# Regrouping tokens 256/512/256 with the samples in the first group, and plain float32 for half of the dense up-projections

## Chip, cores and metric

One core of a Trainium2 chip runs the whole program. The metric is device time in microseconds, the median of three runs. Engines are called TensorE (PE, with its weight loads PEld), VectorE (DVE), ScalarE (ACT), GpSimd (POOL) and SyncE (SP, which issues most DMAs).

## The reference

One inference step of a one-layer decoder for a prompt of 1024 tokens and for 32 samples (8 sequences of 4 new tokens), all in float32, with the same weights. A token mixer (a gated delta rule with a recurrent state, and three groups of dilated window attention), attention over a memory of 256 entries, and PEER, a layer of 16384 experts of which each token picks 8 x 16:

```
def layer(h, conv_buf, s0, wins, kv, g_mix, ...):
    mix, ... = token_mixer(rmsnorm(h, g_mix), conv_buf, s0, wins, w_in, ..., w_out)
    h = h + mix
    h = h + mem_attend(rmsnorm(h, g_memq), kv, w_mq, w_mo)
    h = h + peer(rmsnorm(h, g_ffn), w_pq, sub_keys, expert_u, expert_v)
...
    # peer, for a block of tokens xb
    q = (xb @ w_pq).reshape(PEER_BLOCK, PEER_HEADS, 2, PEER_DHALF)
    s = einsum('thpc,hpnc->thpn', q, sub_keys);  sv, si = top_k(s, 16)
    cand = sv[:, :, 0, :, None] + sv[:, :, 1, None, :];  cv, ci = top_k(cand, 16)
    eid = i1 * PEER_NKEYS + i2;  gate = softmax(cv)
    hid = gelu(einsum('thkd,td->thk', expert_u[eid], xb))
    out = einsum('thk,thkd->td', gate * hid, expert_v[eid])
```

The samples have own states: a recurrent matrix and convolution rows for each sequence, window caches of 128, 512 and 2048 positions, and a memory cache. They are outputs too, shifted by the new tokens.

## The kernel before

Tokens go through in three groups: 384, 384 and 256 prompt tokens; the 32 samples ride with the second group (SG = 1, n = 416 columns). For each group `base(gi)` runs norm, projections (activations are kept transposed, 128 model rows by n tokens), convolutions, delta blocks of 128 tokens, the three window groups, `w_out`, memory attention and the norm before PEER; then `peer_route` picks experts (top 16 twice for each of 8 heads, on VectorE, one round for each block of tokens). Group 0 splits each operand into a high and a low float32r part (`split`: one ScalarE copy, one VectorE subtraction) and multiplies three products; groups 1 and 2 use plain float32 matmuls. `wtile` loads a weight pair of 2 x 512 KB and calls `sprinkle`, which advances the generator `self.gate` by some steps.

PEER is done in two ways. Sparse tokens (group 0, and 192 tokens of group 2) gather their expert rows: `experts` issues one indirect DMA of 128 rows of 4 KB for each slot on GpSimd, and VectorE takes a dot product (L1257) or adds a scaled row (L1406). That is 576 slots for `expert_u` and 576 for `expert_v`, four blocks of 128 and one half block (64 tokens folded to 128 rows, `peer_rest`). They are traced at the very end; `mm` notes an anchor instruction on VectorE after each `rate` columns of matmul (float32 counted four times), and `paced` ties one gather step behind each anchor, so that the gathers spread over the rest of the kernel. RATES give the columns per anchor by stage.

Dense tokens (group 1 with its samples, and 64 of group 2: ND = 480) go through all experts. `gate_matrix` builds, for 32 tokens at a time, a matrix of gates over 128 x 128 experts from two one-hot matrices (L1299 and L1306 on VectorE, L1305 and L1308 on ScalarE, four matmuls for four tokens, L1313 copies them out) and writes it to DRAM (`gscr`). `expert_up` computes Gelu of one group of 128 experts for all dense tokens: load 512 KB, split, 24 matmuls of 480 columns (three products of eight chunks), Gelu (L1330). 60 of the 128 groups are done ahead and parked in DRAM (`uscr`); the loop in `dense` reads those back or computes the others, multiplies by gates, splits, and does 24 matmuls for the down-projection into seven PSUM accumulators. `finish_T` adds, norms and writes.

A scheduler orders the traced instructions on each engine by the order of tracing, and pulls later ones forward where an engine would be idle and their buffers (SBUF tags and PSUM tags with a fixed number of slots) are free. The order is fixed when the kernel is built; each engine then runs its own in order. Of the eight PSUM banks `ps` has 2, `tp` (transposes) 2, `po` 1 and `dl` 3.

Order before: base 0 with the memory's K/V, route 0; base 1; route 1 and then the gate matrix of group 1, stepped on by the weight loads of base 2 (STEPS); base 2; then, in `dense`, the split operand is loaded, the 60 early up-projections are traced with route 2 and the gate matrix of the 64 tokens stepped between them (PACE); then the dense loop.

Of the kernel before, what the change touches and what calls it, by code (L numbers as in the profile page):

```python
# [27 lines left out]
GI = 4  # L28
STEPS = (2, 4)
PACE = (1, 1, 1, 1, 1, 1, 1, 1, 1, 1, 1, 1, 1)  # L30
RATES = (4000, 3900, 2000, 3700)
EARLY = 60
NDT = 9
# [4 lines left out]
TD = 4  # L38
GROUPS = ((0, 384), (384, 384), (768, 256))
SG = 1  # L40
EX = 64
N1 = 384 + NS
ND = N1 + EX
KEPT = 256 - EX
COPIES = 3
# [86 lines left out]
class Kern:  # L132
# [36 lines left out]
    def p(self, shape, tag="ps", dt=F32):  # L169
        self.uid += 1  # L170
        bufs = {"ps": 2, "tp": 2, "po": 1, "dl": 3}[tag]
        return self.ps.tile(list(shape), dt, tag=tag, name=f"{tag}_{self.uid}", bufs=bufs)
# [18 lines left out]
    def setup(self):  # L191
        nc, I = self.nc, self.I
        self.x0 = self.t((P, KD, GROUPS[0][1]), "O", 1)
        self.load_x(0, self.x0)
        cf = self.const.tile([P, CF_N], F32, name="cf")
        nc.sync.dma_start(cf, I["cf"])
        self.C = {n: cf[:, o:o + w] for n, (o, w) in CF_OFF.items()}
        cb = self.const.tile([P, CB_N], BF16, name="cb")
        nc.gpsimd.dma_start(cb, I["cb"])
        self.CB = {n: cb[:, o:o + w] for n, (o, w) in CB_OFF.items()}  # L200
        identb = self.const.tile([P, P], BF16, name="identb")
        nc.vector.tensor_copy(identb, self.C["ident"])
        self.identb = identb
        gains = self.const.tile([P, 5, KD], F32, name="gains")
        nc.sync.dma_start(gains, I["gains"])
# [24 lines left out]
        self.hscr = self.dr.tile([SEQ, D], F32, name="hscr")  # L230
        self.fscr = self.dr.tile([SEQ, D], F32, name="fscr")
# [31 lines left out]

    def operand(self, a, n, kn=KD, tags=(("fr", 1, 2), ("acc", 1, 2), ("vzs", 1, 2), ("oh", 1, 2))):
        if self.gi:
            return ([a[:, k] for k in range(kn)],)
        hi, lo, k = [], self.t((P, kn, n), "A", 1, F32R), 0
        for tag, bufs, m in tags:
            m = min(m, kn - k)
            if m:  # L270
                x = self.t((P, m, n), tag, bufs, F32R)
                self.split(a[:, k:k + m, :n], x, lo[:, k:k + m, :n])
                hi += [x[:, j] for j in range(m)]
                k += m
        return hi, [lo[:, k] for k in range(kn)]
# [10 lines left out]
    def sprinkle(self, k):  # L286
# [3 lines left out]
        self.calls += 1  # L290
        for _ in range(k if k > 100 else STEPS[self.calls > 9]):
            next(self.gate, None)
# [129 lines left out]
    def delta_in(self, gi, L, n, h, a, stc, ncv, qk_all, vz_all, vzs, ssp):  # L422
# [14 lines left out]
        if gi == 0:  # L437
            for b in range(nb):
                nc.tensor.transpose(zp[:, b], zT[:, b * P:(b + 1) * P], C["ident"])
        for b in range(nb + smp if gi else 0):  # L440
# [720 lines left out]
    def peer_route(self, gi, L, n, f, hres):  # L1161
# [5 lines left out]
        self.spare = "dtm", NDT, 512  # L1167
        eid, gate = self.t((P, 8, nt, 16), "eid", 2, I32), self.t((P, nt, 8, 16), "gate", 2)
        for h in range(8):
# [98 lines left out]

    def gate_dense(self, route):
        nc, C = self.nc, self.C  # L1270
        yield from route
        yield from self.gate_matrix(self.picks[1], 0, 0, lambda: [self.t((P, P, UT), "C", 1)])

    def gate_extra(self):
        yield from self.gate_matrix(self.picks[2][1:], P - EX, N1 // UT, lambda: [self.t((P, P // 2, UT), x, 1) for x in "OA"])

    def gate_matrix(self, picks, skip, out, tiles):
        nc, C = self.nc, self.C
        for eid, gate in picks:
# [12 lines left out]
            yield  # L1292
            for sub in range(skip // UT, m // UT):
                st = tiles()
                nu = P // len(st)
# [21 lines left out]
                out += 1  # L1317

    def expert_up(self, e, fh, fl):
        nc = self.nc  # L1320
# [12 lines left out]
    def dense(self, route):  # L1333
        nc, I = self.nc, self.I
        fl, fh = self.t((P, KD, ND), "B", 1, F32R), self.t((P, KD, ND), "C", 1, F32R)
        last = self.t((P, ND), "vzs", 1)
        for k in range(KD):
            x = self.tmp((P, ND))
            nc.sync.dma_start(x, self.tscr[0, :, k])
            self.split(x, fh[:, k], fl[:, k])  # L1340

        self.rate = RATES[2]
        side = chain(route, self.gate_extra())
        early = {e: i for i, e in enumerate(e for e in range(P) if e * EARLY // P != (e + 1) * EARLY // P)}
        for e, i in early.items():
            for _ in range(PACE[i // 4] if i % 4 == 0 and i // 4 < len(PACE) else 0):
                next(side, None)
            nc.sync.dma_start(self.uscr[i], self.expert_up(e, fh, fl))
        for _ in side:
            pass  # L1350
        self.rate = RATES[3]
        gs = self.t((P, 2, ND // UT, GI, UT), "A", 1)
        gs = [gs[:, j] for j in range(2)]
        wx = self.t((P, 2, 2, ND), "O", 1, F32R)
        accs = [self.p((P, ND), tag) for tag in ("tp", "tp", "dl", "dl", "dl", "po", "ps")]

# [65 lines left out]
    def finish_T(self, h):  # L1422
        t0, L = GROUPS[1]
        self.norm_T(self.ks(h), 4, ND, self.ks(h))
        for b in range(L // P):
            self.rows(h, b * P, P, self.O["y_p"], t0 + b * P)
        self.rows(h, L, NS, self.O["y_s"], 0)
        if EX:
            self.rows(h, N1, EX, self.O["y_p"], SEQ - EX)

    def store_rows(self, src, gi, scr):
        t0, L = GROUPS[gi]
        for c0 in range(0, KEPT if gi else L, P):
            self.rows(src, c0, min(P, KEPT - c0) if gi else P, scr, t0 + c0)

# [10 lines left out]
    def base(self, gi):  # L1446
# [30 lines left out]
        if smp:  # L1477
            self.zq = [c[:, 3072:].rearrange("p (b t) -> p b t", b=8)]
        def windows(i):
# [35 lines left out]
        self.norm_T(self.ks(h), 3, n, self.ks(f))  # L1515
        if gi:
            o, c0 = (0, 0) if gi == 1 else (N1, KEPT)
            for x, y in enumerate((f, h)):
                if c0 < n:
                    nc.sync.dma_start(self.tscr[x, :, :, o:o + n - c0], y[:, :, c0:])  # L1520
        if gi != 1:
            self.store_rows(f, gi, self.fscr)
# [4 lines left out]
    def peer(self, gi, sel):  # L1527
        nc, O = self.nc, self.O
        t0, L = GROUPS[gi]
        for b in range((KEPT if gi else L) // P):  # L1530
            r0 = t0 + b * P
# [7 lines left out]
    def peer_rest(self, eid, gate):  # L1539
        nc = self.nc  # L1540
        m, r0 = KEPT % P, SEQ - P
        parts = P // m
# [16 lines left out]
        self.finish(acc[:m], self.O["y_p"][r0:r0 + m])  # L1559

    def run(self):
# [3 lines left out]
        for gi in range(3):  # L1565
            route = self.base(gi)
            if gi == 2:
                self.sprinkle(1000)
                self.finish_T(self.dense(route))
                break  # L1570
            if gi == 0:
                for _ in route:
                    pass
                self.work, self.anchors = 0, []
            else:
                self.calls = 0
                self.rate = RATES[1]
                self.gate = self.gate_dense(route)
        self.paced(chain(self.peer(0, self.picks[0]), self.peer(2, self.picks[2]), self.peer_rest(*self.picks[2][1]) if KEPT % P else ()))

# [99 lines left out]
```

## Time and profile before

| | |
|---|---|
| runs | 4074.78 us median, 4065.51 to 4086.79 |
| span of the profiled execution | 4081.0 us, the only time that it has of its own |
| TensorE busy | 3619.0 us, 89% |
| VectorE busy | 2938.5 us, 72% |
| ScalarE, GpSimd busy | 36% each |
| DMA | 1101.38 MB, mean 270 GB/s |
| HBM | 1025.37 MB read, 117.02 MB written |

Busy times are shares of the span. Matmuls overlap in the record, so the duration of one is longer than the distance to the next; where pace matters, the length of a run of equal matmuls is divided by their number. A plain float32 product appears as two instructions, a float32r product as one. The granted clock is a share of TensorE's full 2.4 GHz.

### The profile page before, as it was taken

The page shows a single profiled execution, that of the slowest core. Times are in us where ns is not written, and L with a number is a line of the kernel's source. Part 1 is how long each engine was busy: PE and PEld are TensorE (multiplying, and loading weights), DVE is VectorE, ACT ScalarE, POOL GpSimd, SP SyncE. Part 2 cuts the span into 40 slices and gives each one's busy share as a digit, 9 for nine tenths or more (in the row PEclk, how much of TensorE's full clock was granted, in tenths as well). Part 3 has the DMA queues.
Part 4 walks back from the last instruction along what each step waited for, and adds up shares of the span by engine and source line. Part 5 has one row for each costly group of instructions (what it writes and reads, how often), then busy time and mean ns, then how long its engine had stood idle before and what let it go on. Part 6 is the DMA issues. An engine that isn't in the chain of part 4 may idle for free.

```text
span 4081.0 us, 54174 instructions
## 1 busy us (share of the span) xinstructions
PE 3619.0 (89%) x18530; PEld 2976.6 (73%) x18530; DVE 2938.5 (72%) x6731; ACT 1470.6 (36%) x3278; POOL 1477.9 (36%) x1317
## 2 busy tenths in 40 slices
PE   8999988888999878774799887899969999999999
PEld 8988878666777634443677776788858888888887
DVE  4422338876575655789977887899768888887886
ACT  4434344333223011211245687223443333333333
POOL 0000000253334545454334443444544444444442
PEclk9998899789878988787788898999989999999998
DMA  6532554376668988886577888999999999999995
GB/s 219 188 117 92 189 196 146 123 254 206 230 229 298 334 331 310 296 297 201 189 237 267 290 321 330 327 349 330 348 323 336 342 342 340 340 339 321 338 332 198
DMA packets 383525, 1101.38 MB, mean 270 GB/s; under 512 B 40528, under 2 KB 147728, under 8 KB 379536
## 3 DMA queue, kind: packets, MB, share of 16 engines
q0 software_dynamic: 168736, 614.54, 42.5%
q1 hardware_dynamic: 214512, 483.37, 33.9%
q8 instruction: 147, 2.41, 0.2%
q14 instruction: 130, 1.06, 0.1%
HBM read 1025.37 MB, written 117.02 MB: 280 GB/s over the span
## 4 chain that ended last, share of the span: by engine, by line
PE 49%; DMA 18%; DVE 14%; issue 10%; POOL 4%; ACT 4%; POOLq 0%; SPq 0%; DVEq 0%; ACTq 0%
PE ps L148 29%; PE dl L148 11%; DMA gat<-expert_u,eid 5%; DMA gat<-expert_v,eid 5%; PE tp L148 4%; POOL gat L1248 4%; PE po L148 3%; DVE gat L1257 2%; DVE acc L1406 2%; DMA gat<-expert_v,e 1%; DMA O<-cmv 1%; PE tp L846 1%; DVE tk L1155 1%; DMA gscr<-C 1%; DVE tmp L419 1%
## 5 line engine op out<-in xcount | busy, mean ns | idle before, releaser
L1248 POOL DMA_INDIRECT gat<-expert_u,eid x512 | 625.1, 1221 | 819.1 <-DVE hid L1257 569.0
L1248 POOL DMA_INDIRECT gat<-expert_v,eid x512 | 627.7, 1226 | 771.8 <-DVE acc L1406 420.3
L1257 DVE CUSTOM_DVE_ANT_0 gat<-gat,fr 128x1024 f32<-128x1024 f32 x576 | 697.1, 1219 | 220.5 <-DMA gat<-expert_u,eid 209.2
L1406 DVE SCALAR_TENSOR_TENSOR acc<-gat,hid,acc 128x1024 f32<-128x1024 f32 x576 | 737.2, 1280 | 146.1 <-DMA gat<-expert_v,eid 128.9
L148 PE MATMUL dl<-dtm,dtm 128*128 128x128 f32 (+3 forms) x2336 | 328.2, 292 | 36.6 <-ACT C L1313 18.1
L148 PE MATMUL ps<-C,w 128*128 128x416 f32 x768 | 309.8, 562 | 43.2 <-DMA w<-w_pq 31.6
L148 PEld LDWEIGHTS dl<-dtm,dtm 128*128 128x128 f32 (+2 forms) x2336 | 307.7, 206 | 54.9 <-ACT C L1313 20.5
L148 PE MATMUL dl<-O,dtm 128*128 128x480 f32 x1152 | 286.3, 379 | 0.0
L148 PEld LDWEIGHTS ps<-C,w 128*128 128x128 f32 x768 | 156.7, 209 | 175.0 <-issue 127.3
L1266 ACT ACTIVATE dtm<-w 128x512 fp32r<-128x512 f32 x288 | 178.0, 629 | 269.7 <-PE dl L148 183.6
L148 PE MATMUL ps<-C,wk 128*128 128x480 f32 x1024 | 249.3, 385 | 21.2 <-ACT C L1266 12.7
L148 PE MATMUL ps<-C,zz 128*128 128x480 f32 (+1 forms) x1088 | 263.1, 379 | 1.4 <-DVE zz L1267 1.4
L1266 ACT ACTIVATE wk<-wv 128x1024 fp32r<-128x1024 f32 x128 | 135.8, 1061 | 332.9 <-PE ps L148 219.8
L148 PE MATMUL ps<-B,wk 128*128 128x480 f32 x1024 | 244.9, 381 | 0.2 <-DVE B L1267 0.2
L148 PEld LDWEIGHTS dl<-O,dtm 128*128 128x128 f32 x1152 | 216.6, 188 | 33.5
L148 PE MATMUL tp<-O,dtm 128*128 128x480 f32 x768 | 208.3, 386 | 32.1 <-ACT O L1266 30.1
L148 PEld LDWEIGHTS ps<-C,wk 128*128 128x128 f32 x1024 | 191.2, 190 | 56.4 <-ACT C L1266 13.6
L148 PEld LDWEIGHTS ps<-C,zz 128*128 128x128 f32 x1088 | 204.1, 188 | 32.3 <-DVE zz L1267 1.8
L1267 DVE TENSOR_TENSOR dtm<-w,dtm 128x512 fp32r<-128x512 f32 x288 | 197.0, 688 | 41.4 <-PE dl L148 16.8
L148 PE MATMUL ps<-A,w 128*128 128x256 f32 (+1 forms) x768 | 197.4, 415 | 21.2 <-ACT tmp L406 13.7
L148 PEld LDWEIGHTS ps<-B,wk 128*128 128x128 f32 x1024 | 193.8, 189 | 30.2 <-DVE B L1267 0.9
L148 PE MATMUL ps<-O,dtm 128*128 128x480 f32 x768 | 210.5, 379 | 0.2 <-DVE vzs L1394 0.2
(479 smaller groups left out, 6665.4 us busy)
## 6 DMA issues: line engine op xcount, KB each, us to landing
wv<-expert_uT SPq DMA_DIRECT2D x128, 512.0 KB
w<-expert_v SPq DMA_DIRECT2D x128, 512.0 KB
w<-w_in SPq DMA_DIRECT2D x102, 512.0 KB
s_win<-cache_win SPq DMA_DIRECT2D x64, 512.0 KB
A<-gscr SPq DMA_DIRECT2D x32, 960.0 KB
gscr<-C SPq DMA_DIRECT2D x13, 2048.0 KB
w<-w_pq SPq DMA_DIRECT2D x48, 512.0 KB
uscr<-tmp SPq DMA_DIRECT2D x60, 240.0 KB
```

Of the source, the lines that this page charges most:

```text
L148: x = self.nc.tensor.matmul(out, lhsT, rhs, **kw)
L419: nc.vector.scalar_tensor_tensor(av, xv(j), cw[:, ch, j:j + 1], av, op0=ALU.mult, op1=ALU.add)
L846: nc.tensor.transpose(tp[:r, c, :], e[:lq, j, o:o + r], C["ident"][:lq, :lq])
L1155: nc.vector.match_replace(out=w, in_to_replace=vals[:, 0:8], in_values=src, imm_value=-3.0e38)
L1248: return self.nc.gpsimd.indirect_dma_start(out=dst, out_offset=None, in_=src, in_offset=bass.IndirectOffsetOnAxis(ap=idx, axis=0))
L1257: nc.vector.tensor_tensor_reduce(out=u, in0=u, in1=fr, scale=1.0, scalar=0.0, op0=ALU.mult, op1=ALU.add, accum_out=hid[:, s:s + 1])
L1266: nc.scalar.activation(hi, x, AF.Copy)
L1267: nc.vector.tensor_tensor(lo, x, hi.bitcast(F32), op=ALU.subtract)
L1406: nc.vector.scalar_tensor_tensor(acc, v, c[:, s:s + 1], acc, op0=ALU.mult, op1=ALU.add)
```

## The change

Groups become 256, 512 and 256, the samples ride with the first (n = 288), and only group 1 is dense: 512 tokens, no samples, nothing of group 2. The sparse tokens are group 0's two blocks, the 32 samples (folded to 128 rows of 32 slots) and group 2's two blocks: 544 slots.

Each group's picks get own buffers (`eid0`, `gate0`, ...). `sprinkle` advances route 1 by one step at each weight load. The gate matrix of group 1 is no longer stepped on in base 2; it is traced after base 2 and route 2, in tiles `B` and `O` + `A` by turns.

Of the 128 up-projections 64 instead of 60 are done ahead, and these by a new function, `expert_fill`: plain float32, 8 products of 512 columns, no splits, from the operand `F` that group 1 left in tile `C`, into an own PSUM bank `fl` (taken from `tp`, which keeps one), with Gelu written over the weight tile. The first 24 use the SBUF tag `vzs` with one slot, the others `wv` with two. They are traced after route 2 and the whole gate matrix. The split operand, in `B` and `C`, is loaded after them.

```
-STEPS = (2, 4)
-PACE = (1, 1, 1, 1, 1, 1, 1, 1, 1, 1, 1, 1, 1)
-RATES = (4000, 3900, 2000, 3700)
-EARLY = 60
+RATES = (4000, 4600, 1500, 3700)
+EARLY = 64
+FILL = 24
...
-GROUPS = ((0, 384), (384, 384), (768, 256))
-SG = 1
-EX = 64
-N1 = 384 + NS
-ND = N1 + EX
-KEPT = 256 - EX
+GROUPS = ((0, 256), (256, 512), (768, 256))
+SG = 0
+ND = GROUPS[1][1]
...
-        bufs = {"ps": 2, "tp": 2, "po": 1, "dl": 3}[tag]
+        bufs = {"ps": 2, "tp": 1, "fl": 1, "po": 1, "dl": 3}[tag]
...
-    def operand(self, a, n, kn=KD, tags=(("fr", 1, 2), ("acc", 1, 2), ("vzs", 1, 2), ("oh", 1, 2))):
+    def operand(self, a, n, kn=KD, tags=(("fr", 1, 3), ("acc", 1, 3), ("oh", 1, 2))):
...
-        for _ in range(k if k > 100 else STEPS[self.calls > 9]):
+        for _ in range(max(k, 1)):
             next(self.gate, None)
...
-        eid, gate = self.t((P, 8, nt, 16), "eid", 2, I32), self.t((P, nt, 8, 16), "gate", 2)
+        eid, gate = self.t((P, 8, nt, 16), f"eid{gi}", 1, I32), self.t((P, nt, 8, 16), f"gate{gi}", 1)
...
-    def gate_matrix(self, picks, skip, out, tiles):
+    def gate_matrix(self, picks):
+        out = 0
...
-            for sub in range(skip // UT, m // UT):
-                st = tiles()
+            for sub in range(m // UT):
+                st = [self.t((P, P // 2, UT), x, 1) for x in "OA"] if out % 2 else [self.t((P, P, UT), "B", 1)]
...
+    def expert_fill(self, e, tag, bufs):
+        nc = self.nc
+        u = self.t((P, KD, P), tag, bufs)
+        nc.sync.dma_start(u, self.I["expert_uT"][e])
+        q = self.p((P, ND), "fl")
+        for k in range(KD):
+            nc.tensor.matmul(q, u[:, k], self.F[:, k], start=k == 0, stop=k == KD - 1)
+        x = u.rearrange("p k e -> p (k e)")[:, :ND]
+        nc.scalar.activation(x, q, AF.Gelu_apprx_tanh)
+        return x
...
     def dense(self, route):
         nc, I = self.nc, self.I
+        self.rate = RATES[2]
+        side = chain(route, self.gate_matrix(self.picks[1]))
+        early = {e: i for i, e in enumerate(e for e in range(P) if e * EARLY // P != (e + 1) * EARLY // P)}
+        for _ in side:
+            pass
+        for e, i in early.items():
+            nc.sync.dma_start(self.uscr[i], self.expert_fill(e, *(("vzs", 1) if i < FILL else ("wv", 2))))
+        self.rate = RATES[3]
         fl, fh = self.t((P, KD, ND), "B", 1, F32R), self.t((P, KD, ND), "C", 1, F32R)
...
-        for e, i in early.items():
-            for _ in range(PACE[i // 4] if i % 4 == 0 and i // 4 < len(PACE) else 0):
-                next(side, None)
-            nc.sync.dma_start(self.uscr[i], self.expert_up(e, fh, fl))
-        for _ in side:
-            pass
-        self.rate = RATES[3]
...
-        accs = [self.p((P, ND), tag) for tag in ("tp", "tp", "dl", "dl", "dl", "po", "ps")]
+        accs = [self.p((P, ND), tag) for tag in ("tp", "fl", "dl", "dl", "dl", "po", "ps")]
...
+        if gi == 1:
             for x, y in enumerate((f, h)):
-                if c0 < n:
-                    nc.sync.dma_start(self.tscr[x, :, :, o:o + n - c0], y[:, :, c0:])
-        if gi != 1:
+                nc.sync.dma_start(self.tscr[x], y)
+            self.F = f
+        else:
             self.store_rows(f, gi, self.fscr)
...
-        self.paced(chain(self.peer(0, self.picks[0]), self.peer(2, self.picks[2]), self.peer_rest(*self.picks[2][1]) if KEPT % P else ()))
+        self.paced(chain(self.peer(0, self.picks[0]), self.peer_rest(*self.picks[0][-1]), self.peer(2, self.picks[2])))
```

## Rows read from the trace of the kernel before

**Rows 1.** The page, busy time of each engine with its share of the span.

```profile
PE 3619.0 (89%) x18530; PEld 2976.6 (73%) x18530; DVE 2938.5 (72%) x6731; ACT 1470.6 (36%) x3278; POOL 1477.9 (36%) x1317
```

**Rows 2.** Busy time by stretch; length, then engines, granted clock, DMA share, GB/s.

```profile
0.00:606.00 606.00, 561.20 (x3267) 511.69 (x3267) 207.76 (x384) 264.21 (x640) 11.47 (x33) 0.92 0.48 168
606.00:890.00 284.00, 237.85 (x1195) 190.40 (x1196) 240.49 (x1058) 105.13 (x219) 72.54 (x98) 0.87 0.50 164
890.00:1390.00 500.00, 453.14 (x2808) 360.90 (x2809) 320.32 (x659) 123.68 (x420) 217.99 (x206) 0.87 0.73 253
1390.00:1660.00 270.00, 220.84 (x880) 128.04 (x880) 156.38 (x239) 43.76 (x114) 125.43 (x104) 0.84 0.90 329
1660.00:2080.00 420.00, 291.88 (x1203) 208.35 (x1202) 372.47 (x1433) 90.15 (x239) 199.92 (x166) 0.81 0.72 243
2080.00:2516.00 436.00, 376.43 (x2351) 318.05 (x2351) 344.63 (x796) 293.29 (x760) 174.69 (x146) 0.87 0.80 284
2516.00:2988.00 472.00, 428.31 (x2066) 368.02 (x2064) 406.31 (x935) 196.31 (x346) 220.32 (x176) 0.97 0.93 337
2988.00:4050.00 1062.00, 1025.86 (x4650) 872.13 (x4651) 881.09 (x1219) 343.03 (x526) 455.53 (x388) 0.98 0.93 331
4050.00:4081.00 31.00, 23.49 (x120) 19.06 (x118) 9.05 (x18) 11.01 (x20) 0.00 (x0) 0.67 0.20 64
```

**Rows 3.** Line L1248, the gathers: duration min/median/max, first and last start.

```profile
L1248 POOL DMA_INDIRECT gat<-expert_u,eid x512: 935/970/3978, 648.6 to 3319.0; - x171
...
L1248 POOL DMA_INDIRECT gat<-expert_v,e x64: 939/1115/2283, 3854.3 to 4021.2; - x64
```

**Rows 4.** Groups of instructions: busy us, mean ns; idle before, releaser.

```profile
L1257 DVE CUSTOM_DVE_ANT_0 gat<-gat,fr 128x1024 f32<-128x1024 f32 x576 | 697.1, 1219 | 220.5 <-DMA gat<-expert_u,eid 209.2
L1406 DVE SCALAR_TENSOR_TENSOR acc<-gat,hid,acc 128x1024 f32<-128x1024 f32 x576 | 737.2, 1280 | 146.1 <-DMA gat<-expert_v,eid 128.9
```

**Rows 5.** The chain that ended last: start us, us, what.

```profile
1218.38 5.74 PE tp L148 x50
...
2864.04 31.21 PE ps L148 x144
```

**Rows 6.** Busy time of the stretch of group 0's delta blocks and windows.

```profile
133.00:457.00 324.00, 312.03 (x1938) 275.91 (x1938) 93.10 (x209) 129.57 (x411) 0.61 (x4) 0.89 0.34 115
```

**Rows 7.** Busy time where the samples' parts ran in group 1.

```profile
1130.00:1200.00 70.00, 63.12 (x457) 51.86 (x457) 53.04 (x114) 15.25 (x51) 25.45 (x27) 0.76 0.62 214
1200.00:1240.00 40.00, 36.95 (x243) 29.17 (x242) 29.25 (x55) 6.95 (x27) 20.59 (x24) 1.00 0.95 358
1340.00:1380.00 40.00, 27.71 (x183) 23.61 (x184) 25.80 (x44) 1.92 (x9) 23.96 (x25) 0.91 0.90 339
1484.00:1570.00 86.00, 51.01 (x308) 24.62 (x308) 39.71 (x72) 16.47 (x47) 32.34 (x28) 0.74 0.93 345
```

**Rows 8.** Timeline of TensorE: start us, us, runs of equal matmuls.

```profile
1034.73 7.85 PE L148 MATMUL ps<-C,w 128*128 128x416 f32 x22
...
2330.81 2.84 PE L148 MATMUL dl<-dtm,dtm 128*128 128x128 f32 x24
```

**Rows 9.** Groups of instructions of the gate matrix, 480 tokens.

```profile
L1306 DVE TENSOR_SCALAR dtm<-cb,i 128x128 f32<-128x128 bf16 x480 | 137.4, 360 | 5.1 <-PE dl L148 4.7
...
L1305 ACT ACTIVATE dtm<-cb,i 128x128 f32<-128x128 bf16 x360 | 112.9, 394 | 1.8 <-PE dl L148 1.7
...
L1299 DVE TENSOR_TENSOR dtm<-cb,i 128x512 f32<-128x512 bf16 x30 | 20.5, 685 | 2.2 <-ACT i L1291 2.2
```

**Rows 10.** Line L1330, the Gelu of an up-projection.

```profile
L1330 ACT ACTIVATE tmp<-ps x128: 545/572/587, 2568.3 to 4037.3; 128x480 f32<-128x480 f32 x128
...
L1330 ACT ACT_TABLE_LOAD  x6: 1283/1283/1283, 2567.0 to 4036.0; - x6
```

**Rows 11.** Group of instructions, the VectorE part of splitting up-projection weights.

```profile
L1267 DVE TENSOR_TENSOR zz<-wv,wk 128x1024 fp32r<-128x1024 f32 x128 | 156.2, 1221 | 49.5 <-ACT wk L1266 49.2
```

**Rows 12.** Tile `tp`, the copy out of a transpose bank.

```profile
L850 ACT ACTIVATE tmp<-tp x124: 204/288/399, 200.9 to 2244.9; 96x192 f32<-96x192 f32 x32, 64x64 f32<-64x64 f32 x32, 96x128 f32<-96x128 f32 x32, 128x256 f32<-128x256 f32 x28
```

More of the change, by code (lines that the diff above doesn't have):

```diff
@@ L192, in setup @@
         nc, I = self.nc, self.I
-        self.x0 = self.t((P, KD, GROUPS[0][1]), "O", 1)
+        self.x0 = self.t((P, KD, GROUPS[0][1] + NS), "O", 1)
         self.load_x(0, self.x0)
@@ L229, in setup @@
         self.vscr = [None] + [self.dr.tile([2, P, 4, 256], F32, name=f"vscr{g}") for g in (1, 2)]
-        self.hscr = self.dr.tile([SEQ, D], F32, name="hscr")
-        self.fscr = self.dr.tile([SEQ, D], F32, name="fscr")
+        self.hscr = self.dr.tile([SEQ + NS, D], F32, name="hscr")
+        self.fscr = self.dr.tile([SEQ + NS, D], F32, name="fscr")
         self.gscr = self.dr.tile([ND // UT, P, P * UT], F32, name="gscr")
@@ L437, in delta_in @@
         if gi == 0:
-            for b in range(nb):
-                nc.tensor.transpose(zp[:, b], zT[:, b * P:(b + 1) * P], C["ident"])
+            for b in range(nb + smp):
+                m = P if b < nb else NS
+                nc.tensor.transpose(zp[:m, b], zT[:, b * P:b * P + m], C["ident"])
         for b in range(nb + smp if gi else 0):
@@ L1267, in split @@
         nc.vector.tensor_tensor(lo, x, hi.bitcast(F32), op=ALU.subtract)
-    def gate_dense(self, route):
+    def gate_matrix(self, picks):
         nc, C = self.nc, self.C
[L1271 to L1275, printed above, removed]
-    def gate_matrix(self, picks, skip, out, tiles):
-        nc, C = self.nc, self.C
+        out = 0
         for eid, gate in picks:
@@ L1340, in dense @@
             self.split(x, fh[:, k], fl[:, k])
-        self.rate = RATES[2]
-        side = chain(route, self.gate_extra())
-        early = {e: i for i, e in enumerate(e for e in range(P) if e * EARLY // P != (e + 1) * EARLY // P)}
-        for e, i in early.items():
-            for _ in range(PACE[i // 4] if i % 4 == 0 and i // 4 < len(PACE) else 0):
-                next(side, None)
-            nc.sync.dma_start(self.uscr[i], self.expert_up(e, fh, fl))
-        for _ in side:
-            pass
-        self.rate = RATES[3]
         gs = self.t((P, 2, ND // UT, GI, UT), "A", 1)
@@ L1426, in finish_T @@
             self.rows(h, b * P, P, self.O["y_p"], t0 + b * P)
-        self.rows(h, L, NS, self.O["y_s"], 0)
-        if EX:
-            self.rows(h, N1, EX, self.O["y_p"], SEQ - EX)
     def store_rows(self, src, gi, scr):
         t0, L = GROUPS[gi]
-        for c0 in range(0, KEPT if gi else L, P):
-            self.rows(src, c0, min(P, KEPT - c0) if gi else P, scr, t0 + c0)
+        for c0 in range(0, L, P):
+            self.rows(src, c0, P, scr, t0 + c0)
+        if gi == SG:
+            self.rows(src, L, NS, scr, SEQ)
     def rows(self, src, c0, m, scr, r0):
@@ L1477, in base @@
         if smp:
-            self.zq = [c[:, 3072:].rearrange("p (b t) -> p b t", b=8)]
+            self.zq = [c[:, 2048:3072].rearrange("p (b t) -> p b t", b=8)]
         def windows(i):
@@ L1515, in base @@
         self.norm_T(self.ks(h), 3, n, self.ks(f))
-        if gi:
-            o, c0 = (0, 0) if gi == 1 else (N1, KEPT)
+        if gi == 1:
             for x, y in enumerate((f, h)):
-                if c0 < n:
-                    nc.sync.dma_start(self.tscr[x, :, :, o:o + n - c0], y[:, :, c0:])
-        if gi != 1:
+                nc.sync.dma_start(self.tscr[x], y)
+            self.F = f
+        else:
             self.store_rows(f, gi, self.fscr)
@@ L1529, in peer @@
         t0, L = GROUPS[gi]
-        for b in range((KEPT if gi else L) // P):
+        for b in range(L // P):
             r0 = t0 + b * P
@@ L1540, in peer_rest @@
         nc = self.nc
-        m, r0 = KEPT % P, SEQ - P
+        m, r0 = NS, SEQ
         parts = P // m
@@ L1558, in peer_rest @@
             nc.vector.tensor_tensor(acc[:m], acc[:m], part, op=ALU.add)
-        self.finish(acc[:m], self.O["y_p"][r0:r0 + m])
+        self.finish(acc[:m], self.O["y_s"])
     def run(self):
@@ L1569, in run @@
                 self.finish_T(self.dense(route))
-                break
-            if gi == 0:
+            elif gi == 1:
+                self.calls, self.gate = 0, route
+            else:
                 for _ in route:
@@ L1574, in run @@
                 self.work, self.anchors = 0, []
-            else:
-                self.calls = 0
                 self.rate = RATES[1]
-                self.gate = self.gate_dense(route)
-        self.paced(chain(self.peer(0, self.picks[0]), self.peer(2, self.picks[2]), self.peer_rest(*self.picks[2][1]) if KEPT % P else ()))
+        self.paced(chain(self.peer(0, self.picks[0]), self.peer_rest(*self.picks[0][-1]), self.peer(2, self.picks[2])))
 def _tiles(w, m=P):
```

## Prediction

> **What bounds the kernel now.** I read the busy shares first, then a table of busy time by stage, then the gathers' first and last starts, then the chain of waits and single lines for prices. The busy shares [rows 1] name no single bound: TensorE 89%, VectorE 72%, the others 36%. The stage table [rows 2] shows why; its boundaries are where one stage's last projection gives way to the next stage's first line. I call 0 to 606 A (base of group 0, no gathers yet: TensorE busy 561 of 606), 606 to 1660 B (route 0 and base of group 1: VectorE 240 of 284 while route 0 runs, then DMA at 0.90 in the last 270), 1660 to 2516 C (route 1, base of group 2 and the gate matrix of 416 tokens: VectorE 717 of 856, TensorE at a granted clock of 0.81 in the first half), 2516 to 2988 D (route 2, 60 early up-projections: TensorE 428 and VectorE 406 of 472), 2988 to 4050 E (the 128 expert groups: TensorE 1026 of 1062, DMA 0.93), and a tail of 31.
>
> Beside all this run 1152 gathers, from 649 to 4021 [rows 3]; each costs VectorE 1.22 us (u) or 1.28 us (v) [rows 4]. That is one per 2.93 us, and the last starts 60 us before the end of the span. So the kernel is a chain of stages with different limits, and gathers that must fit into them.
>
> **Stage A: samples in, one block of 128 out.** The split matmul runs 144 of 480 columns in 31.21 us [rows 5], 217 ns each or 0.451 ns a column: 173 ns at 384 columns, 130 at 288, 231 at 512. A has 448 chunk products (w_in 272, w_out 48, w_mq and w_mo 64 each) times three: 1344 x 43 ns = 58 us leave. One of three delta blocks leaves too. The stretch with three blocks, windows and memory K/V took 324 us [rows 6], 108 a block; the windows of dilation 4 and 16 keep their four residue blocks at any group length, so I count half, 54 us. In come the samples' parts. Where they ran in B they show as stretches [rows 7]: 70 us for the recurrent part, two of 40 us for windows, 86 us for the memory cache at 345 GB/s, shared with gathers. In A no gather runs. The 16.8 MB of memory cache at the full 345 GB/s take 49 us; the recurrent part I leave at 70; the window matmuls go 50 in 5.74 us [rows 5], so 560 take 64 us. Sum in: 183. A = 606 + 183 - 58 - 54 = 677. Bounds: half of what comes in hidden, 586; the four stretches of rows 7 added whole (236) and the block saving nothing, 784.
>
> **Stage B: samples out, 128 prompt tokens in.** Out go the same stretches, 70 + 40 + 40 + 86 = 236 us [rows 7], which lie in one line with base 1. In comes a delta block: the 500 us from 890 to 1390 hold three blocks with windows beside 70 + 40 + 40 of samples, 117 a block, and half of that, as in A, is some 60. Plain float32 issues two instructions a product: 22 of 416 columns in 7.85 us [rows 8], 0.35 us each with the first one's fill off, hence 0.43 at 512. 448 x 2 x 0.08 = 72 us more; TensorE does not set the end of all of B, so I take 40 (bounds 0 and 72). B = 1054 - 236 + 60 + 40 = 918. Route 0 still has three rounds per head (two blocks and 32 samples), so its VectorE part stays. Bounds 818 (nothing comes back) and 1000 (only the last 270 us, the stretch limited by DMA, get shorter).
>
> **Stage C: gate matrix out.** C is set by VectorE, 717 of 856, 84%. The gate matrix of 480 tokens costs VectorE 137.4 + 20.5 us and ScalarE 113 in its commonest form [rows 9]; 416 of the 480 lie in C: 137 us of VectorE. At 84% that is 163 us of time. Route 1 keeps four rounds a head, now one head per weight load instead of two; that moves nothing off VectorE and I price it at 0 (a gain if it lets base 2 start sooner, up to 50). Into C come the first 24 plain up-projections, in an own SBUF buffer and an own PSUM bank: 16 instructions x 0.43 = 6.9 us each, 165 us of TensorE. What hides them is TensorE's room: busy 668 of 856 at clocks of 0.81 and 0.87, less some 95 us for the gate matrix's matmuls (104 times 8, of which 24 go in 2.84 us [rows 8]). If that cover is gone they cost up to 165. Each Gelu among Exp and Silu can cost two table loads of 1.283 us [rows 10]: 24 x 2.6 = 62 us of ScalarE, which has 383 of 856 busy; bounds 0 and 62 on the path, I take 0. C = 856 - 163 = 693, rounded 690. Bounds 640 and 790.
>
> **Stage D: the gate matrix and the plain up-projections.** Out go 60 split up-projections: 60 x 24 x 217 ns = 312 us of TensorE and 60 x 1.22 = 73 us of VectorE [rows 11]. In come 448 more tokens of gate matrix (512 for 64): VectorE 448/480 x 158 = 147, TensorE 105 (112 times 8 at the same pace), and ScalarE work that took 293 us together with the rest of the second half of C [rows 2], so it fits; and 40 plain up-projections, TensorE 275, no VectorE. VectorE: 406 - 73 + 147 = 480, at this stage's own 86% 558 us. TensorE: 428 - 312 + 105 + 275 = 496, under it. D = 560. Bounds 500 (gathers thin out, VectorE freer) and 714 (all 64 here, below).
>
> **Stage E.** Down and remaining up-projections: before, 196 x 24 x 217 = 1021 us within 1062, 41 over. After, 128 + 64 = 192 x 24 x 231 = 1064, with the 41 1105. New at its head: the split operand goes into the buffer that the plain operand held, so it waits for the last plain up-projection; eight loads and splits, some 15 us beside what D had of that. E = 1120. DMA falls a little: four blocks and 32 slots are 544 slots for 576, 64 gathers of 512 KB fewer.
>
> **Sum.** 677 + 918 + 690 + 560 + 1120 + 31 = 3996, 85 under the span of 4081.0. The profiled span lies 6 us over the median of the runs, 4074.78, and inside their 4065 to 4087, so on the median's scale 3990, -2.1%.
>
> **Gathers.** They start with route 0 behind A, near 649 + 71 = 720. The last of 1088 at 2.93 us starts at 3908, some 90 us before the end. Anchors are fewer in B and C (one per 4600 columns for 4000 and 3900) and denser in D.
>
> **One rule beside it.** Transposes get one PSUM bank for two. [Rows 12] show the copy that frees a bank: 124 of some 0.29 us. A cycle of copy and release unhidden would be about 0.5 us, the 0.29 and as much again for hand-over as an estimate; 128 window and 16 memory tiles make 72 us. I count 0 because delta and projection matmuls of the same stage stand between. The Trainium skill, Perfetto Trace Analysis, section Matmuls, says that independent matmul groups should rotate through several banks so that the emptying of one lies under the next group; by it the 72 us would be paid and the sum would be 4062. No row of this kernel has a single transpose bank, so the trace does not settle it.
>
> **Rivals.** (1) The gathers end last: slower. For: anchors thin by 15 to 18% in B and C, and the stream starts 71 us later. Against: 64 fewer, denser anchors in D. The last gather, its sum, norm and store need some 40 us. At 3.1 us each, 720 + 1088 x 3.1 + 40 = 4133. It decides from 2.97 us a gather on, where 720 + 1088 x 2.97 + 40 = 3991, the forecast's own end; what goes beyond adds 1.1 us for each ns.
> (2) The plain up-projections do not get into C but all into D. TensorE in D: 428 - 312 + 105 + 64 x 6.9 = 663, and the single bank adds Gelu's 0.57 [rows 10] and a hand-over to each, 64 x 0.8 = 51: 714. D = 714, the end 150 later at 4150. For: they are traced last, with the lowest rank. Against: the gathers are traced last too and run from 649 on. The Trainium skill, FP8 and Floating Point Precision, section TensorE Precision Notes, counts four passes for true FP32, against the three products of the split; it speaks against the plain form, and with four thirds of 5.55 us it would make it 7.4, not 6.9 us: 32 us on 64.
> (3) The single transpose bank: 4062, no measurable change.
> (4) A takes the samples unhidden, A = 784: 4097. For: TensorE is already busy 561 of 606 there.
> (5) More gain: B 860 and C 640, 3880. For: those stages have TensorE at 0.81 to 0.87 clock and waits of DMA that go away.
>
> **Numbers.** A measurement of this kernel tells about 0.5% from no change: 4054 to 4095. Forecast 0.50 (own range 3920 to 4055), (1) 0.08, (2) 0.10, (3) 0.11, (4) 0.09, (5) 0.12. Faster: 0.47 + 0.12 + about half of (3) and little of (4), 0.65. Same: the rest of (3), part of (4) and of the forecast, 0.14. Slower 0.21. The stages' bounds are about 90 us either way for A, B and C, 60 for D, 25 for E; taken as independent they make 170, eight tenths of that 130: 3860 to 4130, which leaves out the far end of (1) and (2).
>
> **What would show it.** A ends between 650 and 700; B is under 950; between the end of A and 2300 stand the plain 512-column matmuls that write the bank fl, at least 20 groups of them; D has VectorE over 80% and TensorE under 95%; E has 24 matmuls per 5.5 us and starts near 2860; the last gather starts before E's last matmul. Wrong would make it: A past 760, D past 650, PE idle on ScalarE's copies of tp tiles, or POOL alone at the end.

## Result and profile after

The changed kernel takes 4238.1 us (median of four runs, 4222.4 to 4251.2) against 4070.5 for the kernel before beside it (4065.5 to 4086.8): ratio 1.0415, 95% interval 1.037 to 1.046. It is slower by 4%, above the upper end of the forecast range. The profiled execution has a span of 4228.4 us, 147 more than before.

The page, busy time by engine (against [rows 1]):

```profile
PE 3840.6 (91%) x18055; PEld 2828.8 (67%) x18055; DVE 2807.1 (66%) x6499; ACT 1465.2 (35%) x3337; POOL 1364.5 (32%) x1255
```

VectorE lost 131 us, as was meant. TensorE gained 222. Busy time by stretch, columns as in [rows 2]; A is the first row, B the next three, C the next three, D two, then E and the tail:

```profile
0.00:670.00 670.00, 601.59 (x4149) 529.55 (x4149) 228.92 (x613) 245.09 (x685) 37.18 (x95) 0.91 0.60 209
670.00:975.00 305.00, 248.59 (x1202) 184.32 (x1202) 260.43 (x1053) 108.55 (x226) 99.41 (x91) 0.85 0.53 176
975.00:1379.00 404.00, 388.40 (x2135) 281.42 (x2134) 202.23 (x389) 126.23 (x402) 113.87 (x97) 0.91 0.51 163
1379.00:1650.00 271.00, 218.58 (x639) 119.28 (x637) 171.79 (x183) 45.81 (x103) 145.15 (x118) 0.85 0.86 300
1650.00:2037.00 387.00, 354.60 (x1212) 205.97 (x1212) 328.07 (x1302) 98.32 (x193) 142.28 (x145) 0.94 0.74 247
2037.00:2331.00 294.00, 269.89 (x1361) 183.11 (x1359) 150.12 (x235) 95.64 (x268) 94.79 (x80) 0.83 0.64 212
2331.00:2610.00 279.00, 266.22 (x1005) 170.66 (x1005) 107.39 (x191) 93.83 (x200) 69.48 (x59) 0.93 0.61 211
2610.00:2880.00 270.00, 249.30 (x900) 150.99 (x901) 224.66 (x775) 101.93 (x228) 103.13 (x93) 0.97 0.87 314
2880.00:3105.00 225.00, 144.78 (x774) 129.02 (x773) 192.00 (x534) 204.85 (x504) 75.40 (x62) 0.75 0.81 285
3105.00:4196.00 1091.00, 1073.45 (x4568) 853.37 (x4569) 925.45 (x1207) 332.36 (x511) 482.68 (x415) 1.00 0.95 334
4196.00:4228.00 32.00, 25.24 (x122) 21.12 (x120) 16.07 (x24) 12.58 (x21) 1.13 (x2) 0.65 0.32 118
```

C is where the forecast is missed most: 960 us for 690 (B takes 62 more than forecast, D and E 65 and 29 less). VectorE in its last 279 us is 38% busy, TensorE 95%. The tile `fl` within C (engine, operation, count: duration in ns min/median/max, first and last start):

```profile
L1315 PE MATMUL fl<-C,vzs x384: 592/592/1223, 1649.9 to 2244.3; 128*128 128x512 f32 x192
...
L1315 PE MATMUL fl<-C,wv x288: 592/592/1221, 2336.2 to 2605.3; 128*128 128x512 f32 x144
```

At 16 instructions each that is 24 plain up-projections in the buffer `vzs` and 18 more in `wv`: 42 in C, not 24. The chain of waits there (start us, us, what) shows how they lie:

```profile
2445.35 7.13 PE fl L1315 x16
2452.48 6.91 PE ps L144 x32
2459.39 2.58 PE fl L1315 x6
2461.96 6.91 PE ps L144 x32
2468.87 4.29 PE fl L1315 x10
2473.16 6.91 PE ps L144 x32
```

TensorE runs without a gap, and group 2's projections (`ps`) wait in its queue behind up-projections that nobody needs before E. In D the gate matrix stands alone in the last 225 us: ScalarE is busy 205, VectorE 192, TensorE 145 at a granted clock of 0.75, and by line 72% of the chain of waits there is ScalarE's.

### The profile page after: what moved, and what is told of

Same layout as the page of the kernel before. It is cut to its first block, busy times and chain, and to the rows that moved or that the text cites. A ratio compares the mean times of both kernels' runs of the same rounds, so it can differ in the third digit from the quotient of the medians.

```text
span 4228.4 us, 52682 instructions
## 1 busy us (share of the span) xinstructions
PE 3840.6 (91%) x18055; PEld 2828.8 (67%) x18055; DVE 2807.1 (66%) x6499; ACT 1465.2 (35%) x3337; POOL 1364.5 (32%) x1255
## 5 line engine op out<-in xcount | busy, mean ns | idle before, releaser
L144 PE MATMUL dl<-dtm,dtm 128*128 128x128 f32 (+2 forms) x2400 | 356.6, 302 | 71.7 <-ACT dtm L1298 34.4
L144 PEld LDWEIGHTS dl<-dtm,dtm 128*128 128x128 f32 (+1 forms) x2400 | 329.5, 214 | 103.7 <-ACT dtm L1298 45.1
L144 PE MATMUL ps<-C,w 128*128 128x512 f32 x768 | 347.1, 608 | 4.7 <-ACT tmp L402 3.8
L1315 PE MATMUL fl<-C,wv 128*128 128x512 f32 x640 | 302.0, 623 | 20.3 <-ACT wv L1317 15.6
L144 PE MATMUL dl<-O,dtm 128*128 128x512 f32 x1152 | 295.2, 391 | 0.0
L1315 PE MATMUL fl<-C,vzs 128*128 128x512 f32 x384 | 193.9, 658 | 24.1 <-DMA vzs<-expert_uT 24.1
L144 PE MATMUL ps<-O,dtm 128*128 128x512 f32 x768 | 207.2, 390 | 0.0
L144 PEld LDWEIGHTS ps<-A,w 128*128 128x128 f32 x768 | 145.3, 193 | 61.8 <-issue 31.6
L144 PEld LDWEIGHTS ps<-O,dtm 128*128 128x128 f32 x768 | 144.3, 188 | 30.4 <-DVE vzs L1392 0.2
L144 PE MATMUL ps<-C,zz 128*128 128x512 f32 (+1 forms) x576 | 153.1, 392 | 0.0
```

Of the source, the lines that this page charges most:

```text
L144: x = self.nc.tensor.matmul(out, lhsT, rhs, **kw)
L1315: nc.tensor.matmul(q, u[:, k], self.F[:, k], start=k == 0, stop=k == KD - 1)
```

## Experiments

Stages of every kernel in us, cut at the same places, with TensorE's busy time on the page; the first row is the prediction's. The cut between D and E is good to some 30 us only: the first down-projection matmul starts at 3012 before (cut at 2988), at 3106 after (3105) and at 3094 in e12 (3115). Where that matters, D and E are taken together.

| kernel | A | B | C | D | E | tail | span | TensorE |
|---|---|---|---|---|---|---|---|---|
| forecast | 677 | 918 | 690 | 560 | 1120 | 31 | 3996 | |
| before | 606 | 1054 | 856 | 472 | 1062 | 31 | 4081 | 3619 |
| after | 670 | 980 | 960 | 495 | 1091 | 32 | 4228 | 3841 |
| e1 | 679 | 984 | 767 | 915 | 1097 | 39 | 4481 | 3920 |
| e2 | 716 | 993 | 774 | 407 | 1118 | 105 | 4113 | 3493 |
| e3 | 661 | 1006 | 903 | 490 | 1117 | 39 | 4216 | 3757 |
| e4 | 610 | 1055 | 889 | 466 | 1060 | 34 | 4114 | 3673 |
| e5 | 664 | 1065 | 757 | 451 | 1063 | 42 | 4042 | 3539 |
| e6 | 663 | 993 | 763 | 971 | 1075 | 32 | 4497 | 3893 |
| e7 | 677 | 999 | 812 | 724 | 1088 | 33 | 4333 | 3867 |
| e8 | 612 | 892 | 794 | 471 | 1079 | 180 | 4028 | 3485 |
| e9 | 675 | 990 | 811 | 625 | 1076 | 31 | 4208 | 3822 |
| e10 | 610 | 1051 | 761 | 448 | 1056 | 101 | 4027 | 3534 |
| e11 | 612 | 1058 | 785 | 450 | 1053 | 87 | 4045 | 3555 |
| e12 | 610 | 1055 | 876 | 574 | 1021 | 33 | 4169 | 3729 |

### The plain up-projections in C (e1, e2)

```
# e1: in dense, around each expert_fill
+            with self.tc.issue_after(last_pe):   # last TensorE instruction of base 2
# e2: in expert_fill
-        q = self.p((P, ND), "fl")
-        for k in range(KD):
-            nc.tensor.matmul(q, u[:, k], self.F[:, k], ...)
...
-        nc.scalar.activation(x, q, AF.Gelu_apprx_tanh)
+        nc.scalar.activation(x, u...[:, ND:], AF.Gelu_apprx_tanh)
```

> All 64 plain up-projections are queued on TensorE behind base 2's last TensorE instruction. Theory 1 (they cost C their TensorE time one for one: 42 of them stood in C, 42 x 6.9 = 290 us): C falls from 960 to about 680, D grows from 495 to 650 to 700 since all 64 (442 us) now stand there, total 4120 to 4160. Theory 2 (C is long for another reason, the single transpose bank or route 1 spread over the weight loads): C stays above 880, D grows all the same, total above 4250.

> The matmuls of the 64 plain up-projections are left out; Gelu reads the second half of the weight tile instead of their sum. Loads, Gelu and stores stay. Theory 1: C about 670, D about 470 (ScalarE and VectorE with the gate matrix), total 3900 to 3960. Theory 2: C above 880, total above 4100.

e1: 4476.7 us, ratio 1.0991 (1.091 to 1.1071); e2, which leaves those matmuls out: 4114.9 (one run). Of e1, C and D:

```profile
1663.00:2430.00 767.00, 644.53 (x2911) 469.38 (x2911) 575.10 (x1723) 213.73 (x586) 303.20 (x280) 0.79 0.70 240
2430.00:3345.00 915.00, 706.94 (x2321) 394.54 (x2319) 573.30 (x1464) 333.00 (x766) 316.42 (x283) 0.89 0.76 269
```

The two C's come to 767 and 774: the 42 up-projections cost C some 190 us, for 42 x 6.9 = 290 us of TensorE. D of e1 missed its expectation: the 64 took 14 us each there, some 22 while the first 24 went through one tile and some 9 for the 40 that had two. In e2 the Gelus have no operand of group 1 left to wait for; the first 24 ran in A, from 360 us on, the other 40 from 2283 on. A grew by 46, which would fit their loads (24 of 512 KB at the 285 GB/s of that stretch are 44 us, an estimate). At e2's end the gathers go on to 4096, 87 us after the dense accumulators are first read, and end last.

### Each half of the change by itself (e3, e12)

e3 takes the groups and the place of the samples from the change and leaves the dense part as before: two transpose banks, 60 split up-projections, the gate matrix stepped on in base 2. e12 keeps the groups of before and makes the 60 early up-projections plain:

```
-            nc.sync.dma_start(self.uscr[i], self.expert_up(e, fh, fl))
+            for k in range(KD):
+                nc.tensor.matmul(q, u[:, k], F[:, k], ...)
+            nc.scalar.activation(x, q, AF.Gelu_apprx_tanh)
...
+        for k in range(KD):     # low half afterwards, in place
+            nc.vector.tensor_tensor(fl[:, k], F[:, k], fh[:, k].bitcast(F32), op=ALU.subtract)
```

> Groups 256/512/256 with the samples in the first, but the dense part as before: two transpose banks, the gate matrix stepped on in base 2, 60 split early up-projections with route 2 between them. Theory 1 (the loss is the plain up-projections in C): A + B as in the changed kernel, 1650; C as before plus 96 more tokens of gate matrix, some 30 us; D shorter by the gate matrix of 64 tokens, some 30; E 45 longer for 512 columns; total 4080 to 4140. Theory 2 (the regrouping is what costs): above 4180.

> The kernel before with its own groups, in which only the 60 early up-projections of stage D become plain float32 (the split's low half is made after them, in place). Theory (TensorE has no room in D, and a plain product costs it more than the three split ones: at 480 columns 16 x 0.40 = 6.4 us for 5.2): D grows from 472 by 50 to 90 us, total 4120 to 4165. Rival (D is set by VectorE, as the prediction had it, 406 of 472 with 60 x 1.22 = 73 us of it for the splits that go): D falls to 400 to 460, total 4010 to 4070.

e3: 4226.3 us, ratio 1.0376 (1.0292 to 1.046). e12: 4153.6, 1.0196 (1.015 to 1.0242). Each half is slower by itself: e3 adds 138 us to TensorE's busy time and 135 to the span, e12 110 and 88 (79 by medians). e3's second theory held, that the regrouping costs: e3 alone is as slow as the whole change (4217.8 to 4234.8 against 4222.4 to 4251.2), and the two halves do not add up to it. Its loss lies in A (55), C (47) and D with E (73); only B gains (48). Windows of e12, the early up-projections and then E:

```profile
2541.00:3115.00 574.00, 523.89 (x1649) 292.56 (x1649) 364.84 (x905) 142.74 (x294) 210.15 (x190) 0.97 0.86 301
3115.00:4136.00 1021.00, 1007.50 (x4566) 857.49 (x4565) 859.49 (x1177) 334.26 (x514) 440.74 (x372) 0.99 0.94 330
```

Against [rows 2], D and E together lost 63 us of VectorE and grew by 61, with 77 more of TensorE. To the first down-projection matmul D grew by 57 (496 to 553; by the table's cut 102). So VectorE at 86% was not what set D of the kernel before.

### The gate matrix in C (e5, e10)

```
# e10; e5 stores a constant tile, which waits for nothing
-        yield from self.gate_matrix(self.picks[1], 0, 0, ...)
+        x = self.picks[1][0][1]
+        for out in range(N1 // UT):
+            yield
+            nc.sync.dma_start(self.gscr[out]..., x[:, None, :].to_broadcast([P, UT, P]))
```

> The kernel before without the gate matrix of its first 416 tokens: a constant tile is stored in its place, so the outputs differ; the last 64 tokens' part stays. Theory of the prediction (stage C is set by VectorE, so the gate matrix's 137 us of VectorE are worth 163 us of time): C falls from 856 to about 693, total about 3910. Rival (the matrix lies in waits of group 2's base and was free there, as the 429 us of that part without plain up-projections already hint): C falls by less than 50 us, total 4030 to 4075.

> The same as the kernel before without the gate matrix of its first 416 tokens, but the stored constant is taken from route 1's choices, so that the stores cannot start before they are known; in the other one they ran at 20 to 95 us of the span and held up the first loads by some 60 us. What that one showed (C shorter by 99 us, not 163 and not under 50): C 740 to 780, A 606, total 3960 to 4000, if the gathers allow it. Rival (the gathers then end last, as they did without the samples): total 4000 to 4040 with a tail of more than 60 us.

e5: 4041.4 us, 0.9916 (0.9887 to 0.9944); e10: 4031.0, 0.9895 (0.9865 to 0.9925). C is 757 and 761: the matrix of 416 tokens is worth 95 to 99 us there, between the two theories. D is shorter too, by 21 to 24: in the kernel before the last two of the matrix's thirteen stores start at 2523 and 2545, in D. To the end of E the matrix is thus worth some 120. Of e10:

```profile
1661.00:2422.00 761.00, 589.05 (x2804) 445.94 (x2804) 554.67 (x1723) 183.74 (x543) 314.05 (x268) 0.81 0.80 271
...
3926.00:4027.00 101.00, 21.28 (x115) 17.12 (x113) 63.55 (x62) 13.47 (x24) 48.66 (x40) 0.56 0.68 227
```

Against the two rows of C in [rows 2], VectorE lost 162 us, TensorE 79, the stage 95. VectorE's idle time grew from 139 to 206, TensorE's hardly moved (188 to 172): a stage set by VectorE would have lost the 162. (50 of them are gathers that left C, 240 for 284; in e5 266 stayed, and C is as short.) The tail says a second thing: with some 100 us less to do before it, the gathers end last.

### One transpose bank (e4, e11, e6)

e4 gives the kernel before one bank `tp` (the other serves only the dense accumulators), e11 does the same to e10. e6 gives the changed kernel two and lets the plain up-projections use `ps`.

```
# e4
-        bufs = {"ps": 2, "tp": 2, "po": 1, "dl": 3}[tag]
+        bufs = {"ps": 2, "tp": 1, "t2": 1, "po": 1, "dl": 3}[tag]
...
-        accs = [... for tag in ("tp", "tp", ...)]
+        accs = [... for tag in ("tp", "t2", ...)]
```

> The kernel before with one transpose bank; the other bank is used by the dense accumulators alone. Theory 3 (the single bank serializes windows and memory attention, 0.5 us for each of some 140 tiles): 72 us longer, 4140 to 4155. Theory 1: within 20 us of the kernel before.

> The same with one transpose bank. Theory (the bank only costs where the gate matrix's matmuls and copies stand between a transpose and its copy; in the two changed kernels whose plain up-projections all ran late, C was 763 with two banks and 767 with one): the same as with two banks within 12 us. Rival (the bank costs 30 to 44 us by itself, as in the kernel before with one bank): C and the total 30 to 44 us longer.

> The changed kernel with two transpose banks again; the plain up-projections take the two banks of the projections instead of one of their own. Theory (the single transpose bank costs here what it costs the kernel before, 44 us): C about 915 instead of 960, total 4185 to 4205. Rival (the bank is a small part here, and sharing the projections' banks makes group 2's base wait for the Gelus): C 960 or more, total 4230 or more.

e4: 4120.5 us, 1.0116 (1.0044 to 1.0188), C longer by 33. e11: 4047.1, 0.9931 (0.9904 to 0.9958), 16 us over e10 and C longer by 24, between the two expectations: part of the price does not need the gate matrix beside it. e6: 4501.0, 1.1043 (1.101 to 1.1077), for another reason: all its up-projections came late, the first Gelu at 2536 where base 2 ends at 2419. (They are traced last, and probably the slots of a shared bank go round in the order of tracing; no run tested that.) That makes it a pair with e1, in which none ran in C either: C 763 with two banks, 767 with one.

```profile
1656.00:2419.00 763.00, 632.56 (x2888) 465.60 (x2887) 568.41 (x1711) 208.05 (x570) 303.89 (x281) 0.81 0.71 241
```

Without up-projections in it the changed kernel's C thus gains little from a second bank; no run had two banks and free up-projections together.

### The samples in B (e8)

The kernel before without the samples' recurrent part, windows and memory cache:

```
-                self.delta_sample(L, qk, vzs, gb, oT)
...
-                self.win_sample(i, self.s_scores(i, L, wq, ks), vs, srun)
...
-            self.win_sample_out(L, srun, oT)
...
-            self.mem_sample(L, mq)
```

> The kernel before without the samples' attention: their recurrent part, window parts and memory cache in group 1 are left out, so the sample outputs differ; the projections still carry their 32 columns. Step of the prediction (the four stretches lie in one line, 236 us): B falls from 1054 to about 818, total about 3845. Rival (part of them lay beside other work; above all the last 270 us of B stay, as they did in the changed kernel): B falls by 120 to 180, total 3900 to 3960.

4035.0 us, 0.99 (0.9866 to 0.9934). B in three parts, and the tail:

```profile
612.00:900.00 288.00, 239.29 (x1194) 191.90 (x1194) 242.83 (x1062) 109.52 (x243) 70.66 (x100) 0.86 0.48 161
900.00:1279.00 379.00, 338.67 (x1928) 262.77 (x1929) 243.58 (x415) 106.76 (x336) 175.77 (x144) 0.86 0.71 238
1279.00:1504.00 225.00, 185.59 (x619) 116.36 (x617) 142.33 (x183) 42.73 (x114) 118.68 (x96) 0.84 0.87 309
...
3848.00:4028.00 180.00, 24.23 (x112) 20.21 (x112) 114.76 (x122) 16.34 (x26) 99.67 (x80) 0.52 0.73 246
```

B falls by 162: 121 in the middle part, 45 in the last, for 236 forecast. TensorE fell by 148 there. C is 62 shorter too, with fewer gathers beside it: 224 start in C for 284, and 284 in B for 316. They come back as a tail of 180, with 78 gathers, so that the total gains 43. Both B and C may have been paying for gathers, and nothing makes those fewer; no run holds their number in a stage fixed.

### Late up-projections (e7, e9)

e7 leaves 17 up-projections free and queues 47 behind base 2, in two tiles and the banks `ps`; e9 in addition lets the late ones write Gelu elsewhere, so that a weight tile is free after its matmuls.

```
+            if i < FILL:          # FILL = 17
+                x = self.expert_fill(e, "vzs", 1)
+            else:
+                with self.tc.issue_after(last_pe):
+                    x = self.expert_fill(e, "wv", 2, "ps")
# e9
+        x = u...[:, :ND] if bank == "fl" else self.tmp((P, ND))
```

> The changed kernel with 17 of the 64 plain up-projections free to run early (as many as stood in the first half of C); the other 47 queue on TensorE behind group 2's base, in two tiles and the projections' two banks. Theory (the plain up-projections between group 2's projections lengthen its chain, and TensorE stands idle in D under the gate matrix): C about 830 instead of 960 (387 and 430 to 450), D 450 to 530 with 47 x 9.5 us = 446 on TensorE beside the gate matrix, total 4080 to 4140. Rival (the gate matrix, with ScalarE busy 205 of 225 us there, does not run beside them): D = 446 + 225 = 670, total about 4280.

> The kernel with seventeen free fills, in which the 47 late plain up-projections write Gelu's result into a tile of its own instead of over their weights. Theory (in D each weight tile goes round load, 16 matmuls, Gelu, store before it is loaded again, some 24 us, so two tiles give one up-projection per 12 us and D 724; TensorE itself needs 6.9 us for one): D falls to 470 to 560, total 4070 to 4170. Rival (D is set by the gate matrix's chain between VectorE, TensorE and ScalarE, which the late up-projections cut into): D stays above 650, total above 4240.

e7: 4315.9 us, 1.0583 (1.0553 to 1.0613): C 812 for some 830 expected, D 724, neither 530 nor 670. Its C:

```profile
1676.00:2488.00 812.00, 724.61 (x3172) 494.90 (x3170) 576.10 (x1711) 232.47 (x607) 291.24 (x279) 0.86 0.70 240
```

Its chain of waits in D (start us, us, what) gave the reason:

```profile
2855.51 6.88 PE ps L1319 x16
2863.04 4.38 DMA uscr<-wv
2867.48 8.08 DMA wv<-expert_uT
```

Matmuls, store, load: the buffer goes round before it can be used again. e9: 4214.0, 1.0349 (1.0311 to 1.0386), D 625. The buffer was worth 99 us. What is left in the middle of D is TensorE:

```profile
2600.00:2700.00 100.00, 98.86 (x435) 60.63 (x434) 97.19 (x339) 91.42 (x211) 27.64 (x26) 1.00 0.83 298
2700.00:2800.00 100.00, 93.56 (x412) 59.52 (x411) 85.59 (x248) 81.58 (x194) 37.69 (x33) 0.95 0.87 327
2800.00:2900.00 100.00, 97.73 (x475) 64.83 (x474) 85.67 (x238) 94.10 (x231) 37.16 (x31) 0.98 0.93 342
```

Gate matrix and up-projections do run side by side there, with TensorE 97% busy; then the rest follow alone, 46 matmuls in 19.90 us on its timeline:

```profile
2999.67 19.90 PE L1319 MATMUL ps<-C,wv 128*128 128x512 f32 x46
```

So against the changed kernel C falls by 149 and D grows by 130 (by 116 to the first down-projection matmul): the 25 up-projections that moved from C to D cost nearly as much there, and the last 201 us of D have TensorE at 78%, with E's first loads and splits at their end.

## Why the prediction was wrong

**What bounds the kernel.** The prediction found "no single bound" and took each stage's limit from its busiest engine. In many runs the time goes with TensorE's busy time: busy +222 and span +147 after the change, +138 and +135 in e3, +110 and +88 in e12, +203 and +127 in e9; -79 and -95 in e10's C, -148 and -162 in e8's B. It is no rule. In e1 and e6 TensorE gained 301 and 274 and the span 400 and 416, as the late up-projections left gaps; in e2 it lost 126 and the span grew by 32, as the gathers end last; and e10 and e1 take 761 and 767 for C with TensorE busy 589 and 645. Nor is busy time work alone: e1 shows 80 us more than the changed kernel for the same 18055 instructions.

The prediction's own terms put 195 us more on TensorE: the split's columns 58 out and window matmuls 64 in (A), 72 in and 64 out (B), 95 out and 165 in (C), 312 out and 380 in (D), 1064 for 1021 (E). 3619 + 195 = 3814 within 3996 would have left it 182 us idle, where before had 462. That sum was never made. (Two slips in its figures change nothing: 104 times 8 matmuls at the row's pace are 98 us, not 95, and E would start at 2845, not 2860.)

**A** came out right, 670 for 677, but no run tested its terms apart. The stretch with the delta blocks and windows took 325 us for 324 before, what follows in A 210 for 149; that the terms add up may in part be luck.

**B, "samples out", the term of 236** was mis-sized: e8 measures 162. The stretches of [rows 7] were cut out of a line in which TensorE, busy 63 of 70 or 37 of 40, also did other work. What comes back, 1054 - 162 to 980, is 88 for the 100 put down; 46 of it lies in B's last part (225 in e8, 271 after), whose projections grew to 512 columns. That term, and not the 40 and 60 beside it, made B 62 too long.

**C, "C is set by VectorE, 717 of 856"**, is the step that failed, in both of its halves. The gate matrix was worth 95 to 99 us of C, not 163 (some 120 with its end in D); in the changed kernel C without any plain up-projection is 767 (e1), 74 over the forecast's 693. And "TensorE's room", which was to hide the plain up-projections, was in good part idle time inside group 2's chain, in which TensorE waited for ScalarE (53 us for L406, 29 for L1178) and for loads of `w_pq` (32). Little of it was to be had: idle time in C is 130 us with no up-projection (e6, 633 of 763), 87 with 17 (e7, 725 of 812) and 69 with 42 (891 of 960). The first 17, beside route 1, took 49 us of time (2.9 each), the other 25 took 148 (5.9 each, of the 6.9 that TensorE needs). Why the first were cheaper is open. The prediction had named that price: "if that cover is gone they cost up to 165". And 42 came, not 24: the later 40 were as free to be pulled forward as the first. 856 - 97 + 190 gives 949 of the 960.

**The bank, counted as 0**, costs the kernel before 44 us by medians (e4), and 16 with the gate matrix gone (e11); next to nothing shows between e1 and e6. The Trainium skill, Perfetto Trace Analysis, section Matmuls, wants independent groups to rotate through several banks; e4 and e11 agree in direction, with the 44 and 16. The 72 that the prediction worked out were too much. In e4 TensorE also shows 54 us more busy for the same 18530 instructions, at a clock of 0.79 in C, so its extra busy time there is not extra work.

**D** ended at 495 for 560. 22 plain up-projections were left in it, not 40 (18 x 6.9 = 124 us of TensorE less), and VectorE was busy 417, not 480, with 150 gathers for 173 in place of the "denser anchors" that the prediction counted on. What was not seen is that the gate matrix, without base 2 around it, is in the main a chain through ScalarE: 225 us with TensorE busy 64% of them. "VectorE 480 us, at this stage's own 86%" took VectorE for the limit; in the kernel before it was not (e12), for the changed kernel's D no run shows it.

**E** was 1091 for 1120. **Plain float32** was priced rightly: 16 x 0.43 = 6.9 us, and 46 in 19.90 us are 0.433 each. The Trainium skill, FP8 and Floating Point Precision, section TensorE Precision Notes, speaks of four passes; by it four thirds of the split's 5.55 would be 7.4, an estimate, and the 6.9 of the row is nearer. The estimate's direction, that the plain form costs TensorE more than the split, agrees with e12: at 480 columns 60 x (16 x 0.406 - 24 x 0.217) = 77 us, and TensorE gained 77 in D and E.

**The rivals.** None was it alone. (2), the up-projections in D, was e1, and 4481 instead of 4150. (1), the gathers, was close behind: after the change they start 3.20 us apart on the mean, not 2.93, the last at 4194, two microseconds before E ends; and in e2, e8, e10 and e11 they end last. The prediction had put its condition at 2.97 us. Of the regrouped kernels none stays under it: e9 has the least, 3.05, by which 720 + 1088 x 3.05 + 40 = 4078. So the forecast's 3990 would probably not have been reached even with C as put down; no run shows how close they can be put.

## What to carry to other kernels

Before any stage is priced, add up what the change puts on the engine that is busiest overall, and see how much idle time the forecast leaves it; a gain that needs that engine at a share it has nowhere shown is doubtful. Idle time inside a chain of dependent steps is no room for other work on an engine that runs its queue in order: what is put in can delay the chain by most of its own length (here by 2.9 and 5.9 us of 6.9). And work spread over the whole kernel, like the gathers here, is only put off where a stage gets shorter, and sets a floor under the total.

## What the runs showed of the hardware

Where up-projections filled TensorE's gaps its granted clock, a mean of parts at 2.4 GHz and parts at 1.2, was higher: 0.81 in the first part of C before [rows 2], 0.94 there after; over the whole of C 0.79 in e1 with none and 0.86 in e7 with 17. That may be part of why the first 17 up-projections were cheap; no run set the clock apart.

In e5 the thirteen constant stores had nothing to wait for and went out from 20 us on, 2 MB each, on the queue of the first weight loads, and A took 664 for 606. In e10 the same stores waited for route 1, and A took 610. Stores that are free too early can cost the loads that everything waits for.
